# Where the stationary weights begin in memory, and in which order the k tiles come, in a two-layer hybrid block on one core

## The chip, the core and the metric

The kernel runs on one core of a Trainium2 chip. The metric is the time of one execution on the device in microseconds (us); the median of several runs counts.

## What is computed

The reference is a block of two layers on 16 meta tokens and 256 tokens of input, 272 together, with a model width of 1024. The zero tokens that pad the sequence to a multiple of 128 in front do not count. In short:

```
for li in range(2):
    hn = rms_norm(h)                       # 272 x 1024
    proj = hn @ w_in[li]                   # 1024 x 13312, split into 12 parts
    o = retention(..), hgrn2(..), diff_attention(..)      # three branches, each 272 x 1024
    y = sum(sigmoid(mg) * (branch @ w_branch[li]))        # three products 1024 x 1024
    h = h + y @ w_out[li]                                 # 1024 x 1024
    u = rms_norm(h) @ w_ffn_in[li]         # 1024 x 5632, then a convolution of width 3 in time
    h = h + (silu(gate) * val) @ w_ffn_out[li]            # 2816 x 1024
out = rms_norm(h)[the 256 input tokens]
```

All is float32. The weights of both layers are some 212 MB and are read once.

## The kernel before

**Products.** Nearly all of TensorE's time goes into the weight products. Features lie on the partitions and tokens in the free dimension, so a weight tile of 128 x 128 is the stationary operand, and the moving operand is a k tile of the activations: 128 features by 272 tokens in layer 0. In layer 1 the last tokens alone matter for the outputs, so most products there move 258 tokens, from token 14 on, which is 56 bytes further (`T0 = 14`). The names in `FULL` (`rk`, `rv`, `hf`, `hi`, `dk`, `dv`) move all 272 there too. To keep float32 accuracy, weights and activations are each cut into a high and a low part of type fp32r, and each weight tile takes three matmuls: `whi` by the high activations (L873), `whi` by the low ones (L874), `wlo` by the high ones (L875). I call these three a triple below.

**Order of tiles.** A product is named by its group and a pair number `j`: `("fi", 3)` makes the output tiles f=0 and f=1 of pair 3. `ORDER` writes out by hand which product follows which, with the background work between. `_turns` turns that into the list of weight tiles: for every k tile in rising order the two columns f=0 and f=1, so 16 triples for the eight k tiles of a product. `fo` has 22 k tiles; its pair 3 runs all k of column 0, then all k of column 1.

- Products of the input projection (`BASE`, 52 pairs a layer, 30 of them short in layer 1) and of the feed-forward input (`fi`, 22 pairs) move the tiles `xh` and `xl`. These are 320 words a k tile apart, so all k tiles begin at the same place modulo 256 bytes: 0, or 56 for the short ones.
- The branch products (`b0`, `b1`, `b2`, 4 pairs each), the output product (`wo`, 4 pairs) and the feed-forward output (`fo`, 4 pairs, layer 0) move tiles cut out of "slots" of four k tiles by 272 words. 272 words are 1088 bytes, so the start moves on by 64 bytes modulo 256 with every k.
- The feed-forward output of the last layer (`final`) is the other way around: 128 tokens of `ghi` and `glo` are stationary and 512 columns of the weights move (L1383 to L1385). There are 22 k tiles, two token tiles and two column halves, three matmuls each: 264 matmuls.

**Weights.** `_Weights.next` brings the weight tiles in chunks of eight, in the order of use: one DMA into `wraw` (3 buffers), one copy on ScalarE into `whi` (rounding to fp32r), one subtraction on VectorE into `wlo` (4 buffers each). `_places` says at which word of `whi` and `wlo` each tile begins. The tile pools put `whi` and `wlo` at 64 modulo 256 and the slots at 64 modulo 256. So a place of 0 means a weight that begins at 64 modulo 256.

**Places before.** Below, the *distance* is the start of the weight minus the start of the moving operand, modulo 256 bytes. In before it is 64 for all of `BASE` with 272 columns, 104 for `BASE` with 258 columns, and 64 (layer 0) or 104 (layer 1) for `b0`, `b1`, `b2`, `wo` and `fo` pairs 0 to 2. For `fi` it is spread by `SPREAD`: pair j has 64 + 16 j for j up to 15, and 72, 112, 152, 192, 232, 16 for the pairs 16 to 21, in both layers alike. In `fo` pair 3 and in `final` the tiles are packed without a wanted place, so the distance takes all of 0, 64, 128 and 192 in turn.

**Order of work.** `_Plan` simulates the engines with a cost for each instruction and writes out the order of all engines; products are its backbone, and the retention, hgrn2 and attention heads are spread behind them. In the feed-forward stage, `Norm.next` makes the normalised `xh` and `xl` anew after four pairs (`DEFER`), while the first pairs are scaled after the product.

Of the kernel before, what the change touches and what calls it, by code (L numbers as in the profile page):

```python
# [19 lines left out]
P = 128  # L20
DEPTH = 2
# [61 lines left out]
def _ktiles(name):  # L83
    return FK if name == "fo" else KD


def _turns(li):

    pairs = [x for x in ORDER if x[0][0] not in MARKS]
    if li == DEPTH - 1:
        pairs = [x for x in pairs if x[0] != "fo"]
    groups = [[x] for x in pairs]
    if li == 0:
        groups[:2] = [pairs[:2]]
    turned = [[x] for n in (BASE, ("fi",)) for x in [x for x in pairs if x[0] in n][DEFER - 1 : DEFER]]
    out = []
    for group in groups:  # L100
        if group == [("fo", 3)]:
            out.append([("fo", 3, k, f) for f in range(2) for k in range(FK)])
        else:
            nk = _ktiles(group[0][0])
            out.append([x + (k, f) for k in range(nk // 2) for x in group for f in range(2)])
            out[-1] += [x + (k, f) for x in group for k in range(nk // 2, nk) for f in range(2)]
            if group in turned:
                out[-1] = out[-1][nk:] + out[-1][:nk]
    if li == DEPTH - 1:
        out.append([("fo", j, k, f) for k in range(FK) for j in range(KD // 2) for f in range(2)])  # L110
    return out
# [12 lines left out]
WIDE = 320  # L124


def _places(depth=DEPTH):

    wants = []
    for li in range(depth):
        for name, j, k, _ in sum(_turns(li), []):
            if name == "fo" and (li == DEPTH - 1 or j == 3):
                wants.append(None)
                continue
            short = li == DEPTH - 1 and name not in FULL
            if name in BASE or name == "fi":
                wants.append((SPREAD[j] + 4 * T0 * short if name == "fi" else APART[short]) % LINE)
                continue  # L140
            wants.append(APART[short] + BLOCK * (name[0] == "b" or name in ("wo", "fo")) + 64 * (k % 4))
    out = []
    for c in range(0, len(wants), CHUNK_TILES):
        at, places = 0, []
        for want in wants[c : c + CHUNK_TILES]:
            if want is not None:
                at += (want // 4 - at) % (LINE // 4)
            places.append(at)
            at += P
        assert at <= ROOM  # L150
        out.append(places)
    return out


def _runs(places):


    runs = []
    for i, at in enumerate(places):
        if runs and at == runs[-1][1] + runs[-1][2] * P:  # L160
            runs[-1][2] += 1
        else:
            runs.append([i, at, 1])
    out = []
    for i, at, n in runs:
        if out and out[-1][4] == n and (out[-1][3] == 1 or at == out[-1][1] + out[-1][2] * out[-1][3]):
            if out[-1][3] == 1:
                out[-1][2] = at - out[-1][1]
            out[-1][3] += 1
        else:  # L170
            out.append([i, at, 0, 1, n])
    return out


# [20 lines left out]
def _stream(w_in, w_branch, w_out, w_ffn_in, w_ffn_out):  # L195

    out = np.empty((DEPTH, STREAM, P, P), np.float32)
    for li in range(DEPTH):
        tiles = sum(_turns(li), [])
        for i, (name, j, k, f) in enumerate(tiles):  # L200
            if name in BASE:
                w, cols = w_in[li], _columns(name, BASE[name] + 2 * j + f)
            elif name in ("b0", "b1", "b2"):
                w, cols = w_branch[li][int(name[1])], _columns(name, 2 * j + f)
            elif name == "wo":
                w, cols = w_out[li], _columns(name, 2 * j + f)
# [6 lines left out]
    out = out.reshape(n, CHUNK_TILES, P, P).transpose(0, 2, 1, 3)  # L213
    return np.ascontiguousarray(out).reshape(n, P, CHUNK_TILES * P)


# [346 lines left out]
class _Weights:  # L563
# [6 lines left out]
        self.used = 0  # L570
        self.places = _places()

    def part(self, t, at, step, runs, n):

        return bass.AP(t.tensor, t.offset + at, [list(t.ap[0]), [max(step, 1), runs], [1, n * P]])

    def next(self):
        c, i = divmod(self.used, CHUNK_TILES)
        self.used += 1
        if i == 0:  # L580
            due = self.plan.key
            room = [P, ROOM]
            raw = self.plan.tile(self.pool, [P, CHUNK_TILES * P], F32, "wraw", 3, f"wraw{c}")
            hi = self.plan.tile(self.pool, room, F32R, "whi", 4, f"whi{c}")
            lo = self.plan.tile(self.pool, room, F32R, "wlo", 4, f"wlo{c}")
            self.plan.key = due - LEAD
            pieces = 1 if c > 1 else 2
            for p in range(pieces):
                n = CHUNK_TILES // pieces
                cols = slice(p * n * P, (p + 1) * n * P)  # L590
                self.sp.dma_start(raw[:, cols], self.w[c][:, cols])
                for first, at, step, runs, each in _runs(self.places[c][p * n : (p + 1) * n]):
                    src = raw[:, (p * n + first) * P : (p * n + first + runs * each) * P].rearrange("p (r x) -> p r x", r=runs)
                    self.act.activation(self.part(hi, at, step, runs, each), src, AF.Copy)
                    self.dve.tensor_tensor(out=self.part(lo, at, step, runs, each), in0=src, in1=self.part(hi, at, step, runs, each).bitcast(F32), op=SUB)
            self.plan.key = due
            self.cut = hi, lo
        hi, lo = self.cut
        at = self.places[c][i]
        return hi[:, at : at + P], lo[:, at : at + P]  # L600

    def chunk(self):

# [13 lines left out]
def _trace(ctx, tc, plan, a, depth, probe):  # L617
# [114 lines left out]
    def x_tile(k, folded):  # L732
        return tuple(t[:, k % 4, :] for t in xs[1 if k >= 4 else 2 if folded else 0])
# [43 lines left out]
    class Norm:  # L777
# [42 lines left out]
        def next(self):  # L820

            self.pairs += 1
            if self.pairs != DEFER + 1:
                return
            self.folded = True
            ys = []
            for k in range(KD):
                plan.key = clock[0] - 12.0 + 0.3 * k
                if k % 4 == 0:
                    ys.append(slot4("y"))  # L830
                y = ys[-1][:, k % 4, :]
# [73 lines left out]
    def split(hi, lo, x):  # L905
        act.activation(hi, x, AF.Copy)
        tt(lo, x, hi.bitcast(F32), SUB)
# [40 lines left out]
    for li in range(depth):  # L948
# [402 lines left out]
        def final():  # L1351
# [21 lines left out]
            for k, t, c in order:  # L1373
# [33 lines left out]
        for name, j in ORDER:  # L1407
# [111 lines left out]
                    norm.finish()  # L1519
            elif name == "fi":  # L1520
                ps = products(lambda k: x_tile(k, norm.folded), name, j, t0)
                if j % 4 == 0:
# [6 lines left out]
                first = META if last else 0  # L1529
                c = temp2("two_b")  # L1530
                for f in range(2):
                    ft = j + f * FK
# [9 lines left out]
                split(st["ghi"][j // 4][:, j % 4, first:], st["glo"][j // 4][:, j % 4, first:], c[:, 0, :])  # L1542
            elif last:
                if j == 0:
                    final()
# [37 lines left out]
```

## Time and profile before

| | |
|---|---|
| median of 3 runs | 1326.98 us (1326.49 to 1327.44) |
| the profiled execution's own time | 1326.42 us |
| its span, first to last instruction | 1324.6 us |
| TensorE matmuls busy | 1314.0 us, 99% |
| VectorE busy | 962.4 us, 73% |
| ScalarE busy | 816.4 us, 62% |
| DMA | 48.0% of 16 engines on the weights' queue |

A matmul's recorded duration is longer than the time from its start to the next one's, since matmuls are pipelined. So the pace is read from starts: two rows of the timeline and the count of triples between them. A span divided by that count is given below as ns a triple.

### The profile page before, as it was taken

The page shows a single profiled execution, that of the slowest core. Times are in us where ns is not written, and L with a number is a line of the kernel's source. Part 1 is how long each engine was busy: PE and PEld are TensorE (multiplying, and loading weights), DVE is VectorE, ACT ScalarE, POOL GpSimd, SP SyncE. Part 2 cuts the span into 40 slices and gives each one's busy share as a digit, 9 for nine tenths or more (in the row PEclk, how much of TensorE's full clock was granted, in tenths as well). Part 3 has the DMA queues.
Part 4 walks back from the last instruction along what each step waited for, and adds up shares of the span by engine and source line. Part 5 has one row for each costly group of instructions (what it writes and reads, how often), then busy time and mean ns, then how long its engine had stood idle before and what let it go on. Part 6 is the DMA issues. An engine that isn't in the chain of part 4 may idle for free.

```text
span 1324.6 us, 28929 instructions
## 1 busy us (share of the span) xinstructions
PE 1314.0 (99%) x11862; PEld 1285.7 (97%) x11862; DVE 962.4 (73%) x1630; ACT 816.4 (62%) x1374; POOL 83.2 (6%) x161
## 2 busy tenths in 40 slices
PE   9999999999999999999999999999999999999998
PEld 8999999999999999999999999999999999999986
DVE  7675777697585789886574757776985867898753
ACT  6847454756576566666456475547565865766643
POOL 5000000001010020000030000000011100200000
PEclk9999999999999999999999999999999999999999
DMA  7544543444544545555555445444445345365653
GB/s 272 194 150 153 172 148 132 140 144 139 181 143 152 183 144 183 183 170 181 175 176 187 149 159 173 148 144 144 148 140 183 136 165 201 131 211 185 204 182 107
DMA packets 60755, 219.07 MB, mean 165 GB/s; under 512 B 6864, under 2 KB 6992, under 8 KB 60624
## 3 DMA queue, kind: packets, MB, share of 16 engines
q1 hardware_dynamic: 60336, 216.71, 48.0%
q8 instruction: 93, 1.52, 0.5%
q10 hardware_dynamic: 288, 0.52, 0.1%
q14 instruction: 38, 0.31, 0.1%
HBM read 216.16 MB, written 1.05 MB: 164 GB/s over the span
## 4 chain that ended last, share of the span: by engine, by line
PE 95%; DVE 3%; ACT 1%; issue 0%; DMA 0%; SPq 0%; DVEq 0%
PE main L873 28%; PE main L875 27%; PE main L874 27%; PE fo L1383 2%; PE fo L1385 2%; PE fo L1384 2%; PE lev L1064 1%; DVE two_b L558 1%; PE ds L1248 1%; PE ms L558 1%; PE do L558 1%; PE ro L558 1%; PE ho L558 1%; PE vt L558 1%; DVE wlo L558 1%; PE s L558 0%
## 5 line engine op out<-in xcount | busy, mean ns | idle before, releaser
L873 PE MATMUL main<-xh,whi 128*128 128x272 f32 (+1 forms) x2368 | 691.8, 292 | 0.7 <-ACT whi L558 0.7
L875 PE MATMUL main<-xh,wlo 128*128 128x272 f32 (+1 forms) x2368 | 676.1, 286 | 1.0 <-DVE wlo L558 0.9
L874 PE MATMUL main<-xl,whi 128*128 128x272 f32 (+1 forms) x2368 | 675.7, 285 | 1.3 <-DVE xl L558 1.3
L558 DVE TENSOR_TENSOR wlo<-wraw,whi 128x1024 fp32r<-128x1024 f32 (+1 forms) x408 | 497.2, 1223 | 197.9 <-ACT whi L558 195.2
L558 ACT ACTIVATE whi<-wraw 128x1024 fp32r<-128x1024 f32 (+1 forms) x408 | 426.4, 1048 | 228.1 <-PE main L874 160.1
L873 PEld LDWEIGHTS main<-xh,whi 128*128 128x128 f32 x2368 | 446.1, 188 | 2.6 <-ACT whi L558 1.1
L874 PEld LDWEIGHTS main<-xl,whi 128*128 128x128 f32 x2368 | 446.1, 188 | 2.3 <-DVE xl L558 1.7
L875 PEld LDWEIGHTS main<-xh,wlo 128*128 128x128 f32 x2368 | 445.7, 188 | 2.4 <-DVE wlo L558 2.3
L558 DVE SCALAR_TENSOR_TENSOR two_b<-main,small,two_b 128x256 f32<-128x256 f32 (+2 forms) x144 | 65.4, 489 | 30.7 <-ACT two_b L558 29.0
L558 ACT ACTIVATE two_b<-main,small 128x272 f32<-128x272 f32 (+1 forms) x72 | 37.2, 566 | 29.6 <-PE main L875 29.6
L558 POOL TENSOR_TENSOR y<-h,rstd 128x272 f32<-128x272 f32 x32 | 34.5, 1113 | 317.7 <-ACT rstd L558 317.7
L875 PE MATMUL main<-ghi,wlo 128*128 128x272 f32 x176 | 51.0, 290 | 0.0
L873 PE MATMUL main<-ghi,whi 128*128 128x272 f32 x176 | 50.9, 289 | 0.0
L874 PE MATMUL main<-glo,whi 128*128 128x272 f32 x176 | 50.2, 285 | 0.0
L558 ACT ACTIVATE vsrc<-main 128x544 f32<-128x544 f32 x24 | 15.0, 625 | 38.5 <-PE main L875 38.4
L873 PE MATMUL main<-b0hi,whi 128*128 128x272 f32 (+1 forms) x128 | 38.2, 298 | 0.0
L873 PE MATMUL main<-b1hi,whi 128*128 128x272 f32 (+1 forms) x128 | 38.1, 298 | 0.0
L875 PE MATMUL main<-b2hi,wlo 128*128 128x272 f32 (+1 forms) x128 | 36.7, 286 | 0.0
L875 PE MATMUL main<-yhi,wlo 128*128 128x272 f32 (+1 forms) x128 | 36.7, 286 | 0.0
L875 PE MATMUL main<-b1hi,wlo 128*128 128x272 f32 (+1 forms) x128 | 36.6, 286 | 0.0
L875 PE MATMUL main<-b0hi,wlo 128*128 128x272 f32 (+1 forms) x128 | 36.6, 286 | 0.0
L873 PE MATMUL main<-b2hi,whi 128*128 128x272 f32 (+1 forms) x128 | 36.5, 285 | 0.0
(244 smaller groups left out, 1934.4 us busy)
## 6 DMA issues: line engine op xcount, KB each, us to landing
wraw<-in_w SPq DMA_DIRECT2D x402, 512.0 KB, 3.3
h<-in_h SPq DMA_DIRECT2D x4, 272.0 KB, 5.7
dec<-in_dec SPq DMA_DIRECT2D x2, 544.0 KB, 5.5
wraw<-in_w SPq DMA_DIRECT2D x4, 256.0 KB, 5.4
const<-in_const SPq DMA_DIRECT2D x1, 937.0 KB, 6.4
gain<-in_gl SPq DMA_DIRECT2D x1, 512.0 KB, 5.2
out<-y ACTq DMA_DIRECT2D x2, 256.0 KB, 2.8
out<-y SPq DMA_DIRECT2D x2, 256.0 KB, 2.7
```

What stands on the lines that cost most here:

```text
L558: self.plan.add(self.name, lambda: f(*args, **kw), cost, outs, ins, args[2] if method == "activation" else None)
L873: nc.tensor.matmul(o, wh, hi, start=first, stop=False)
L874: nc.tensor.matmul(o, wh, lo, start=False, stop=False)
L875: nc.tensor.matmul(o, wl, hi, start=False, stop=last)
L1064: nc.tensor.matmul(o, keys, x, start=True, stop=True)
L1248: nc.tensor.matmul(ss[m][:, at : at + nk], q[half, hd, q0 : q0 + P], k[half, hd, :nk], start=True, stop=True)
L1383: nc.tensor.matmul(o, gh, wh, start=False, stop=False)
L1384: nc.tensor.matmul(o, gl, wh, start=False, stop=False)
L1385: nc.tensor.matmul(o, gh, wl, start=False, stop=end)
```

## The change

1. All `fi` products get the distance that `BASE` has: 64 with 272 columns. `SPREAD` goes.
2. All short products of layer 1 (258 columns) get the distance 160: `BASE`, `fi`, `b0`, `b1`, `b2` and `wo`.
3. `b0`, `b1`, `b2`, `wo` and `fo` take their k tiles downward in blocks of four (3, 2, 1, 0, 7, 6, 5, 4, ...); `wo` ends with 5, 4, 7, 6. Going from one k to the next, the start of weight and moving operand goes back by 64 bytes instead of on by 64. `fo` pair 3 gets the distance 64 too.
4. In the last layer `ghi` and `glo` hold 256 tokens a k tile instead of 272, so that every stationary tile of `final` begins at 64 modulo 256 and the distance is 0 throughout.
5. The buffers of `whi` and `wlo` shrink from 4608 to 4352 bytes (both multiples of 256), and within a chunk the tiles are stored sorted by place, so that ScalarE and VectorE still write most chunks by one instruction.

```diff
+def _ks(name):
+    ks = list(range(_ktiles(name)))
+    if name in BASE or name == "fi":
+        return ks
+    blocks = [ks[i : i + 4][::-1] for i in range(0, len(ks), 4)]
+    if name == "wo":
+        blocks[-1] = [5, 4, 7, 6]
+    return sum(blocks, [])
...
-            out.append([("fo", 3, k, f) for f in range(2) for k in range(FK)])
+            out.append([("fo", 3, k, f) for f in range(2) for k in _ks("fo")])
...
-            out.append([x + (k, f) for k in range(nk // 2) for x in group for f in range(2)])
-            out[-1] += [x + (k, f) for x in group for k in range(nk // 2, nk) for f in range(2)]
+            ks = _ks(group[0][0])
+            out.append([x + (k, f) for k in ks[: nk // 2] for x in group for f in range(2)])
+            out[-1] += [x + (k, f) for x in group for k in ks[nk // 2 :] for f in range(2)]
...
-APART = (0, 96)
+BEGIN = 64
 BLOCK = 64
-ROOM = CHUNK_TILES * P + 2 * LINE // 4
+ROOM = CHUNK_TILES * P + LINE // 4
...
-SPREAD = [16 * i for i in range(16)] + [8 + 40 * i for i in range(6)]
+APART = (64, 160)
...
             if name in BASE or name == "fi":
-                wants.append((SPREAD[j] + 4 * T0 * short if name == "fi" else APART[short]) % LINE)
-                continue
-            wants.append(APART[short] + BLOCK * (name[0] == "b" or name in ("wo", "fo")) + 64 * (k % 4))
+                moving = [0, 0]
+            else:
+                moving = [BLOCK + 4 * T * (k % 4)] * 2
+            wants.append([APART[short] + 4 * T0 * short - BEGIN + x for x in moving])
...
+        if c // CHUNK_TILES > 1 and None not in mine:
+            order.sort(key=lambda i: mine[i][0] % LINE)
...
-                gh, gl = (x[k // 4][:, k % 4, tokens(t)] for x in (hi, lo))
+                gh, gl = (x[k // 4][:, k % 4, t * P : (t + 1) * P] for x in (hi, lo))
...
-                    st.setdefault("ghi", []).append(slot4("ghi", F32R))
-                    st.setdefault("glo", []).append(slot4("glo", F32R))
+                    for n in ("ghi", "glo"):
+                        g = slot(n, F32R)[:, : 4 * (T - first)]
+                        st.setdefault(n, []).append(g.rearrange("p (a t) -> p a t", a=4))
```

On TensorE, POOL and SP the order of instructions is row for row what it was (names and shapes; start addresses and the number of a k tile do not show there). On ScalarE and VectorE it is the same but for four chunks, all of them in layer 0's feed-forward output. On ScalarE, before, the chunks at the end of `fo` pair 2 and the beginning of pair 3 (`whi` is the rounded copy of a chunk's raw weights):

```order
L558 ACTIVATE whi_1213<-wraw_1212 128x4x256
L558 ACTIVATE whi_1216<-wraw_1215 128x256
L558 ACTIVATE whi_1216<-wraw_1215 128x768
L558 ACTIVATE whi_1222<-wraw_1221 128x1024
L558 ACTIVATE whi_1225<-wraw_1224 128x1024
```

And the same place after:

```order
L589 ACTIVATE whi_1213<-wraw_1212 128x4x256
L589 ACTIVATE whi_1216<-wraw_1215 128x2x128
L589 ACTIVATE whi_1216<-wraw_1215 128x2x256
L589 ACTIVATE whi_1216<-wraw_1215 128x2x128
L589 ACTIVATE whi_1222<-wraw_1221 128x4x256
L589 ACTIVATE whi_1225<-wraw_1224 128x4x256
```

The chunk 1216 is written in three pieces instead of two, and the chunks of pair 3 behind it in four blocks with gaps of 64 bytes by one instruction; their neighbours stay. On VectorE the same chunks, before (`wlo` is the subtraction):

```order
L558 TENSOR_TENSOR wlo_1214<-wraw_1212,whi_1213 128x4x256
L558 TENSOR_TENSOR wlo_1217<-wraw_1215,whi_1216 128x256
L558 TENSOR_TENSOR wlo_1217<-wraw_1215,whi_1216 128x768
L558 TENSOR_TENSOR wlo_1223<-wraw_1221,whi_1222 128x1024
L558 TENSOR_TENSOR wlo_1226<-wraw_1224,whi_1225 128x1024
L558 TENSOR_TENSOR h_78<-h_78,main_1199 128x544
```

And after:

```order
L589 TENSOR_TENSOR wlo_1214<-wraw_1212,whi_1213 128x4x256
L589 TENSOR_TENSOR wlo_1217<-wraw_1215,whi_1216 128x2x128
L589 TENSOR_TENSOR wlo_1217<-wraw_1215,whi_1216 128x2x256
L589 TENSOR_TENSOR wlo_1217<-wraw_1215,whi_1216 128x2x128
L589 TENSOR_TENSOR wlo_1223<-wraw_1221,whi_1222 128x4x256
L589 TENSOR_TENSOR wlo_1226<-wraw_1224,whi_1225 128x4x256
L589 TENSOR_TENSOR h_78<-h_78,main_1199 128x544
```

The pieces are the same as on ScalarE. In all, each of the two engines has three instructions more; the same bytes are written.

More of the change, by code (lines that the diff above doesn't have):

```diff
@@ L117 @@
 LINE = 256
[L118 removed]
+BEGIN = 64
 BLOCK = 64
[L120 removed]
+WIDE = 320
+ROOM = CHUNK_TILES * P + LINE // 4
 T0 = META - 2
 FULL = ("rk", "rv", "hf", "hi", "dk", "dv")
[L123 to L124 removed]
+APART = (64, 160)
 def _places(depth=DEPTH):
@@ L133, in _places @@
         for name, j, k, _ in sum(_turns(li), []):
-            if name == "fo" and (li == DEPTH - 1 or j == 3):
+            if name == "fo" and li == DEPTH - 1:
                 wants.append(None)
@@ L145, in _places @@
[L145 to L151, printed above, removed]
-    return out
[L155 to L171, printed above, removed]
+        mine = wants[c : c + CHUNK_TILES]
@@ new lines, in _places @@
+        order, places = list(range(CHUNK_TILES)), [[0] * CHUNK_TILES for _ in range(2)]
+        if c // CHUNK_TILES > 1 and None not in mine:
+            order.sort(key=lambda i: mine[i][0] % LINE)
+        for part in range(2):
+            at = 0
+            for i in order:
+                if mine[i] is not None:
+                    at += (mine[i][part] // 4 - at) % (LINE // 4)
+                places[part][i] = at
+                at += P
+            assert at <= ROOM, at
+        out.append((order, places))
@@ new lines, in _places, with _boxes, box @@
+    return out
+def _boxes(*places):
+    def box(first, n):
+        for inner in (n, 2, 1):
+            if n % inner:
+                continue
+            dims = []
+            for at in places:
+                at = at[first : first + n]
+                one = at[1] - at[0] if inner > 1 else P
+                two = at[inner] - at[0] if inner < n else 0
+                if one < 1 or two < 0 or any(at[i] != at[0] + i // inner * two + i % inner * one for i in range(n)):
+                    break
+                dims.append((at[0], two, one))
+            if len(dims) == len(places):
+                return first, n // inner, inner, dims
+        return None
+    out, first, end = [], 0, len(places[0])
+    while first < end:
+        found = next(x for n in range(end - first, 0, -1) if (x := box(first, n)))
+        out.append(found)
+        first += found[1] * found[2]
@@ L212, in _stream @@
     n = DEPTH * STREAM // CHUNK_TILES
-    out = out.reshape(n, CHUNK_TILES, P, P).transpose(0, 2, 1, 3)
+    out = out.reshape(n, CHUNK_TILES, P, P)
+    out = np.stack([out[c, order] for c, (order, _) in enumerate(_places())])
+    out = out.transpose(0, 2, 1, 3)
     return np.ascontiguousarray(out).reshape(n, P, CHUNK_TILES * P)
@@ L571, in __init__, with part @@
         self.places = _places()
-    def part(self, t, at, step, runs, n):
-        return bass.AP(t.tensor, t.offset + at, [list(t.ap[0]), [max(step, 1), runs], [1, n * P]])
+    def part(self, t, at, two, one, outer, inner):
+        return bass.AP(t.tensor, t.offset + at, [list(t.ap[0]), [max(two, 1), outer], [one, inner], [1, P]])
     def next(self):
@@ L591, in next @@
                 self.sp.dma_start(raw[:, cols], self.w[c][:, cols])
[L592 to L595, printed above, removed]
+                order, places = self.places[c]
+                mine = [[x[i] for i in order[p * n : (p + 1) * n]] for x in places]
+                for first, outer, inner, dims in _boxes(*mine):
+                    src = self.part(raw, (p * n + first) * P, inner * P, P, outer, inner)
+                    to_hi, to_lo = (self.part(t, *x, outer, inner) for t, x in zip((hi, lo), dims))
+                    self.act.activation(to_hi, src, AF.Copy)
+                    self.dve.tensor_tensor(out=to_lo, in0=src, in1=to_hi.bitcast(F32), op=SUB)
             self.plan.key = due
             self.cut = hi, lo
-        hi, lo = self.cut
-        at = self.places[c][i]
-        return hi[:, at : at + P], lo[:, at : at + P]
+        return tuple(t[:, at[i] : at[i] + P] for t, at in zip(self.cut, self.places[c][1]))
     def chunk(self):
@@ L1521, in _trace @@
                 ps = products(lambda k: x_tile(k, norm.folded), name, j, t0)
+                first = META if last else 0
                 if j % 4 == 0:
-                    st.setdefault("ghi", []).append(slot4("ghi", F32R))
-                    st.setdefault("glo", []).append(slot4("glo", F32R))
+                    for n in ("ghi", "glo"):
+                        g = slot(n, F32R)[:, : 4 * (T - first)]
+                        st.setdefault(n, []).append(g.rearrange("p (a t) -> p a t", a=4))
                 u = ps
@@ L1528, in _trace @@
                     evacuate(u, ps)
-                first = META if last else 0
                 c = temp2("two_b")
@@ L1541, in _trace @@
                 tt(c[:, 0, :], c[:, 0, :], c[:, 1, :], MUL)
-                split(st["ghi"][j // 4][:, j % 4, first:], st["glo"][j // 4][:, j % 4, first:], c[:, 0, :])
+                split(st["ghi"][j // 4][:, j % 4, :], st["glo"][j // 4][:, j % 4, :], c[:, 0, :])
             elif last:
```

1 line of the change is left out of this document (removed).

## The prediction

> **What bounds the kernel now.** I read the page first, then the chain of waits, then the starts of matmuls in the timeline.
>
> ```profile
> span 1324.6 us, 28929 instructions
> PE 1314.0 (99%) x11862; PEld 1285.7 (97%) x11862; DVE 962.4 (73%) x1630; ACT 816.4 (62%) x1374; POOL 83.2 (6%) x161
> PEclk9999999999999999999999999999999999999999
> PE 95%; DVE 3%; ACT 1%; issue 0%; DMA 0%; SPq 0%; DVEq 0%
> PE main L873 28%; PE main L875 27%; PE main L874 27%; PE fo L1383 2%; PE fo L1385 2%; PE fo L1384 2%; PE lev L1064 1%; DVE two_b L558 1%; PE ds L1248 1%; PE ms L558 1%; PE do L558 1%; PE ro L558 1%; PE ho L558 1%; PE vt L558 1%; DVE wlo L558 1%; PE s L558 0%
> ```
>
> TensorE's own work is 95% of the chain that sets the end, at full clock, and the three matmuls of a triple are 82% of it. So a nanosecond taken from every triple counts in full, except where another engine holds the chain. The number of matmuls and columns does not change here; what can change is the pace. The next rows are starts of TensorE's matmuls; between two of them lies a known number of triples.
>
> ```profile
> 685.92 0.28 PE L873 MATMUL main<-xh,whi 128*128 128x272 f32 x1
> 709.61 0.29 PE L873 MATMUL main<-xh,whi 128*128 128x258 f32 x1
> 732.24 0.28 PE L873 MATMUL main<-xh,whi 128*128 128x272 f32 x1
> ```
>
> These are `hf` (272 columns, distance 64) and then `hg` (258 columns, distance 104) in layer 1, four pairs or 64 triples each, with nothing between: 23.69 / 64 = 370.2 ns and 22.63 / 64 = 353.6 ns a triple. The `fi` products have the same shapes and other distances:
>
> ```profile
> 517.08 0.28 PE L873 MATMUL main<-xh,whi 128*128 128x272 f32 x1
> 547.25 0.29 PE L873 MATMUL main<-xh,whi 128*128 128x272 f32 x1
> 553.27 0.29 PE L873 MATMUL main<-xh,whi 128*128 128x272 f32 x1
> 607.62 0.29 PE L873 MATMUL main<-ghi,whi 128*128 128x272 f32 x1
> 1138.46 0.28 PE L873 MATMUL main<-xh,whi 128*128 128x258 f32 x1
> 1144.22 0.28 PE L873 MATMUL main<-xh,whi 128*128 128x258 f32 x1
> 1157.67 0.28 PE L873 MATMUL main<-xh,whi 128*128 128x258 f32 x1
> 1163.47 0.28 PE L873 MATMUL main<-xh,whi 128*128 128x258 f32 x1
> 1169.07 0.29 PE L873 MATMUL main<-xh,whi 128*128 128x258 f32 x1
> 1238.17 0.28 PE L873 MATMUL main<-xh,whi 128*128 128x258 f32 x1
> ```
>
> In layer 0, pairs 7 to 21 (240 triples) run from 517.08 to 607.62: 377.3 ns a triple, 7.1 more than at distance 64. Pair 12 alone (547.25 to 553.27, distance 0) takes 376.3. In layer 1, pairs 5 to 18 (224 triples, 1157.67 to 1238.17) take 359.4; pair 5 (distance 144) takes 362.5, pair 6 (1163.47 to 1169.07, distance 160) takes 350.0, pair 2 (1138.46 to 1144.22, distance 96) takes 360.0. The work around these pairs on the other engines is the same, and the distance alone differs. So the distance sets the pace, by up to 12 ns a triple, and the two distances that the change gives (64 with 272 columns, 160 with 258) are the fast ones seen.
>
> The Trainium skill's page "TensorE: Matmul & The Clock Gate" (section "Step-by-step: what each phase is for") says that TensorE has two independent read ports into its memory, one for the moving operand and one for weights, and that loading the next weights takes no bandwidth from the running matmul. By it no start address would matter and the sum below would be 0. The rows 350.0 and 362.5 for equal shapes speak against it; it stands below as a rival.
>
> **The change part by part.** The sum is made against the profiled execution's 1326.42 us, of which 1324.6 is span; it lies 0.56 below the median of 1326.98.
>
> *`fi`, layer 0.* Here other engines hold the chain for a while:
>
> ```profile
> 482.84 0.15 PE main L874
> 483.01 1.07 ACT whi L558
> 503.77 1.15 DVE wlo L558
> 504.96 0.39 PE main L875
> 1135.56 0.13 PE main L874
> 1135.71 1.07 ACT whi L558
> 1153.96 0.42 DVE xl L558
> 1154.43 0.39 PE main L874
> ```
>
> and in the list of waits:
>
> ```profile
> PE main L874 <- DVE xl L558: 1.3, 1, 1.3
> ```
>
> The chain of waits goes through ScalarE and VectorE from 483.0 to 505.0, where VectorE makes `wlo`, the convolutions and the new `xl` one behind the other. A faster TensorE only waits longer there, so what is gained between is lost. Pairs 6 to 21 come behind it: 256 triples x 7.1 = 1.8 us. Before 483.0 lie pair 0, which has distance 64 already, and some 9 triples of pair 1: at up to 10 ns 0.1. Together 1.9.
>
> *`fi`, layer 1.* The chain is off TensorE from 1135.7 to 1154.4, with an open wait of 1.3 us for `xl`. Before that lie pair 0 (distance 64) and half of pair 1; I take the 10 ns of pair 2 for pair 0: 0.2 us. Behind it come pairs 5 to 21, 272 triples, from 359.4 to 350.0: 2.6 us. Just after the wait there is something else:
>
> ```profile
> 1155.14 0.31 PE L873 MATMUL main<-xh,whi 128*128 128x258 f32 x1
> 1157.53 0.30 PE L875 MATMUL main<-xh,wlo 128*128 128x258 f32 x1
> ```
>
> 18 matmuls of pair 4 (distance 128), the first and last of which are shown, start 2.39 / 17 = 141 ns apart, against 117 at distance 160. The clock is full there; this distance has a second, slower pace into which the long wait has thrown it. Without it, 18 x 24 = 0.4 us. Together 3.2 us; I keep 3.1, since the last pairs have some other work between.
>
> *`BASE` with 258 columns.* 30 pairs x 16 = 480 triples, from 353.6 to the 350.0 of pair 6 of `fi`, whose residues are exactly theirs after: 1.7 us. Some of these triples have background matmuls between (`lev`, `ds`, `ro` and others in the chain's lines), where the pace starts anew; I take 1.5. The single pair of 16 triples is all that bears this price, so its ends are 0 and 1.9.
>
> *`b0` to `b2`, `wo` and `fo`, steady part and steps.* Here each k has two triples (f=0, f=1), then comes a step to the next k.
>
> ```profile
> 425.61 0.29 PE L873 MATMUL main<-b2hi,whi 128*128 128x272 f32 x1
> 473.50 0.28 PE L873 MATMUL main<-xh,whi 128*128 128x272 f32 x1
> 1080.62 0.29 PE L873 MATMUL main<-b2hi,whi 128*128 128x258 f32 x1
> 1126.59 0.28 PE L873 MATMUL main<-xh,whi 128*128 128x258 f32 x1
> ```
>
> `b2` and `wo` (128 triples in each layer) take 47.89 / 128 = 374.1 ns in layer 0 and 45.97 / 128 = 359.1 in layer 1. Against the steady 370.2 and 353.6 at the same distances, a step costs twice the difference: 7.8 and 11.0 ns. In a step upward the next weight, which is loaded while the last matmul of the old k runs, lies 128 (layer 0) or 168 (layer 1) from that matmul's moving operand; downward it lies at 0 or 96. No row of before shows a downward step. Its lower price is that one matmul at the pace of these distances: (376.3 - 370.2) / 3 = 2.0 and (360.0 - 350.0) / 3 = 3.3 ns; as the upper one I set twice today's, 16 and 22. I take the middle of the lower price and today's, 5 and 7, since the distance in the step is a better one but the step stays a break. Layer 0 has 16 pairs x 8 + 3 pairs x 22 = 194 steps: 194 x 2.8 = 0.5 us (ends 1.1 and -1.6). Layer 1 has 256 triples and 128 steps: from 359.1 to 350.0 + 3.5 = 353.5, so 256 x 5.6 = 1.4 us (ends 1.9 and -0.5). In `fo` pair 3 the spread distances go and every triple has a step: I set 0.1.
>
> The new order makes nothing late: the halves of `y` and the blocks of four are finished together, and `wo` still reaches k 6 and 7 as its last four triples. The weights come in the same chunks at the same times, so SP's queue is not touched.
>
> *`final`.* Its 22 k tiles have 12 matmuls each; the distance goes 64, 128, 192, 0 and again.
>
> ```profile
> 1257.12 0.39 PE L1383 MATMUL fo<-whi,ghi 128*128 128x512 f32 x1
> 1265.46 0.39 PE L1383 MATMUL fo<-whi,ghi 128*128 128x512 f32 x1
> 1268.19 0.40 PE L1383 MATMUL fo<-whi,ghi 128*128 128x512 f32 x1
> 1301.41 0.40 PE L1383 MATMUL fo<-whi,ghi 128*128 128x512 f32 x1
> ```
>
> k 0 to 15 (192 matmuls) take 44.29 / 192 = 230.7 ns each; k 3, at distance 0, takes 2.73 / 12 = 227.5. At distance 0 throughout: 264 x 3.2 = 0.8 us (ends 0.5 and 0.9).
>
> *Writing the weights.* Three more instructions on each of ScalarE and VectorE, all in `fo` of layer 0, where the page has these two busy to 73% and 62% and TensorE waits for neither: nothing. If that cover were gone, each would cost no more than the fixed part of such an instruction, some tenths of a microsecond. The pools keep their residues, since the buffers shrink by 256 bytes.
>
> The sum: 1.9 + 3.1 + 1.5 + 0.5 + 1.4 + 0.1 + 0.8 = 9.3 us, so 1317.1 for a profiled execution and **1317.7 us** for the median.
>
> **The rivals.**
>
> (a) *The 160 does not carry over.* The good pace of one pair of `fi` is its own, and `BASE`, the branch products and `wo` in layer 1 keep what they have. For it: distance 104 gives 353.6 in `hg` but 359.1 where k steps. Against it: within `fi` the paces of 64 and of 160 hold over all 16 triples, and `BASE` gets the same bytes of both operands. Loss 1.5 + 1.4: 1320.6 us. Chance 0.15.
>
> (b) *The feed-forward stages turn VectorE-bound.* TensorE asks for weights 2 to 3% sooner, and the waits of 483 to 505 and 1136 to 1154 come again. Against it: behind 505 and 1154.4 the chain is TensorE's. If all of `fi`'s 5.0 us went back: 1322.7 us. Chance 0.07.
>
> (c) *Slower: downward steps lock the slow pace.* The 141 ns above show that a distance can hold a run at 24 ns a matmul more once it is thrown in. If each downward step did that for the two triples of its k, 6 x 24 = 144 ns would come on each of 322 steps, 46 us: with 11 us of gains in the other parts some 1362 us. The point from which it decides: the other parts bring 1.9 + 3.1 + 1.5 + 0.8 = 7.3, and free steps would bring 2.9 more and the steady part of layer 1 0.9; steps of more than some 35 ns eat all of it. Against it: no clean run of products shows more than 11 ns a step. Chance 0.03.
>
> (d) *Addresses do not matter*, and something else set those paces: 1327.0 us, no change. Against it are the rows; for it nothing here. Chance 0.02. This is what the Trainium skill's page named above would give.
>
> **How the numbers follow.** The forecast has 0.73. The range takes in (a), the ends of the steps, and half of (b) below: gains of 4.5 to 12 us, 1315.0 to 1322.5. What a measurement of this kernel can tell from no change is some 0.2%, 2.7 us: faster than that in the forecast, (a), (b) and most of what lies between, 0.93; within it 0.04 ((d) and a costly step); slower 0.03 (c).
>
> **What would show it.** In the profile after, `fi` of layer 0 should run at 370 ns a triple, `fi` and `BASE` of layer 1 at 350, `b2` and `wo` at 372 to 373 and near 353.5, `final` at 227.5 a matmul; the wait for `xl` in layer 1 should grow from 1.3 to some 1.7 us (10 ns on some 40 triples of pairs 1 to 4 before it), and the run at 141 ns should be gone. I am wrong if `b2` and `wo` stand above 374 and 359, or if `BASE` with 258 columns stays at 353.6.

## The result, and the profile after

| | before | after |
|---|---|---|
| median | 1326.57 us (1326.30 to 1327.44, 6 runs) | 1318.11 us (1317.66 to 1318.42, 6 runs) |
| ratio, 95% interval | | 0.9937 [0.9927, 0.9947] |
| the profiled execution's own time | 1326.42 us | 1318.42 us |
| its span | 1324.6 us | 1316.6 us |

The changed kernel is faster by 8.5 us; the prediction for its median was 1317.7. From the page after, the span, the engines, the granted clock and the chain by engine:

```profile
span 1316.6 us, 28935 instructions
PE 1305.5 (99%) x11862; PEld 1278.1 (97%) x11862; DVE 962.9 (73%) x1633; ACT 816.9 (62%) x1377; POOL 83.5 (6%) x161
PEclk9999999999999999999999999999999999999999
PE 96%; DVE 2%; ACT 1%; DMA 0%; issue 0%; SPq 0%; DVEq 0%
```

The same 11862 matmuls at the same full clock take 8.5 us less of TensorE's time; VectorE and ScalarE have three instructions more each and are otherwise where they were. The next rows are starts of TensorE's matmuls in the changed kernel, at the places that the prediction showed of before, with the first column the start in us.

```profile
425.15 0.28 PE L905 MATMUL main<-b2hi,whi 128*128 128x272 f32 x1
472.86 0.29 PE L905 MATMUL main<-xh,whi 128*128 128x272 f32 x1
516.34 0.29 PE L905 MATMUL main<-xh,whi 128*128 128x272 f32 x1
605.14 0.29 PE L905 MATMUL main<-ghi,whi 128*128 128x272 f32 x1
682.98 0.29 PE L905 MATMUL main<-xh,whi 128*128 128x272 f32 x1
706.67 0.28 PE L905 MATMUL main<-xh,whi 128*128 128x258 f32 x1
729.07 0.29 PE L905 MATMUL main<-xh,whi 128*128 128x272 f32 x1
1076.04 0.28 PE L905 MATMUL main<-b2hi,whi 128*128 128x258 f32 x1
1098.60 0.28 PE L905 MATMUL main<-yhi,whi 128*128 128x258 f32 x1
1121.35 0.28 PE L905 MATMUL main<-xh,whi 128*128 128x258 f32 x1
1157.87 0.28 PE L905 MATMUL main<-xh,whi 128*128 128x258 f32 x1
1158.13 0.39 PE L907 MATMUL main<-xh,wlo 128*128 128x258 f32 x1
1163.65 0.28 PE L905 MATMUL main<-xh,whi 128*128 128x258 f32 x1
1250.20 0.40 PE L1415 MATMUL fo<-whi,ghi 128*128 128x512 f32 x1
1293.73 0.39 PE L1415 MATMUL fo<-whi,ghi 128*128 128x512 f32 x1
```

Paces first. `fi` of layer 0, pairs 7 to 21: 88.80 us for 240 triples, 370.0 ns (377.3 before). `hf`, whose distance was not changed: 23.69 / 64 = 370.2, as before. `hg`: 22.40 / 64 = 350.0 (353.6). `b2` and `wo` of layer 0 together: 47.71 / 128 = 372.7 (374.1). In layer 1 `b2` has 22.56 / 64 = 352.5 and `wo` 22.75 / 64 = 355.5 (both together 359.1). `final`, k 0 to 15: 43.53 / 192 = 226.7 a matmul (230.7).

Then the stretches between these rows, against the same ones of before. The eight microseconds of the span lie in them as follows:

| stretch | before | after | gain | predicted |
|---|---|---|---|---|
| start to `fi` of layer 0 | 473.50 | 472.86 | 0.64 | some 0.3 (steps) |
| `fi` of layer 0 | 134.12 | 132.28 | 1.84 | 1.9 |
| `fo` of layer 0, start of layer 1 | 78.30 | 77.84 | 0.46 | some 0.3 (steps, pair 3) |
| `hf` to the last product before `b2`, layer 1 | 394.70 | 393.06 | 1.64 | 1.5 + 0.7 |
| `b2`, `wo`, layer 1 | 45.97 | 45.31 | 0.66 | 0.7 |
| `fi` of layer 1 | 130.53 | 128.85 | 1.68 | 3.1 |
| `final` to the end of the span | 67.48 | 66.40 | 1.08 | 0.8 |
| sum | 1324.6 | 1316.6 | 8.0 | 9.3 |

The predicted column divides the 1.4 of layer 1's `b0` to `b2` and `wo` by halves, and the 0.5 + 0.1 of layer 0 likewise. The gain of the first row is not the change's; the same start of `BASE` products in both profiles, before and after:

```profile
35.30 0.29 PE L873 MATMUL main<-xh,whi 128*128 128x272 f32 x1
```

```profile
34.67 0.28 PE L905 MATMUL main<-xh,whi 128*128 128x272 f32 x1
```

Up to here no distance has changed, and after is already 0.63 us ahead: scatter of the start. Some 0.2 of it is lost again among products of layer 0 that the change does not touch, so that 0.4 is left at the start of `b1`; `b2` and `wo` brought 47.89 - 47.71 = 0.18 by themselves. So of the 8.0 some 7.6 is the change's.

The waits of TensorE in the changed kernel (in us: total, times, longest):

```profile
PE main L906 <- DVE xl L589: 2.0, 2, 1.6
PE main L907 <- DVE wlo L589: 0.8, 3, 0.3
```

In before the wait for `xl` was 1.3 in one piece. The run at 141 ns behind it is gone, and another thing stands there: from 1157.87 to 1163.65 the sixteen triples of pair 6 take 361 ns each, with a late matmul at 1158.13, and the pairs after it do not come back to 350 in this execution: they run at 353.

### The profile page after: what moved, and what is told of

Same layout as the page of the kernel before. It is cut to its first block, busy times and chain, and to the rows that moved or that the text cites. A ratio compares the mean times of both kernels' runs of the same rounds, so it can differ in the third digit from the quotient of the medians.

```text
span 1316.6 us, 28935 instructions
## 1 busy us (share of the span) xinstructions
PE 1305.5 (99%) x11862; PEld 1278.1 (97%) x11862; DVE 962.9 (73%) x1633; ACT 816.9 (62%) x1377; POOL 83.5 (6%) x161
## 4 chain that ended last, share of the span: by engine, by line
PE 96%; DVE 2%; ACT 1%; DMA 0%; issue 0%; SPq 0%; DVEq 0%
PE main L905 28%; PE main L907 27%; PE main L906 27%; PE fo L1417 2%; PE fo L1416 2%; PE fo L1415 2%; PE lev L1096 1%; PE ds L1280 1%; PE ms L589 1%; PE do L589 1%; PE ro L589 1%; PE ho L589 1%; PE vt L589 1%; DVE two_b L589 1%; DVE wlo L589 1%; PE s L589 0%
## 5 line engine op out<-in xcount | busy, mean ns | idle before, releaser
L905 PE MATMUL main<-yhi,whi 128*128 128x272 f32 (+1 forms) x128 | 36.4, 284 | 0.0
L906 PE MATMUL main<-b0lo,whi 128*128 128x272 f32 (+1 forms) x128 | 36.4, 284 | 0.0
L906 PE MATMUL main<-b1lo,whi 128*128 128x272 f32 (+1 forms) x128 | 36.4, 284 | 0.0
```

The source lines that it names most:

```text
L905: nc.tensor.matmul(o, wh, hi, start=first, stop=False)
L906: nc.tensor.matmul(o, wh, lo, start=False, stop=False)
```

## The experiments

**Steps upward again** (e1_up): the k tiles of the branch products, `wo` and `fo` rise as in before; all distances stay.

```diff
-    blocks = [ks[i : i + 4][::-1] for i in range(0, len(ks), 4)]
-    if name == "wo":
-        blocks[-1] = [5, 4, 7, 6]
-    return sum(blocks, [])
+    return ks
```

> The changed kernel with all k tiles in rising order again; distances stay 64 and 160. Theory (what the next weight's distance is in a step sets the step's cost): b2 and wo in layer 0 go back from 372.5 and 372.9 to about 374.1 ns a triple; in layer 1 the next weight lies 224 from the moving operand in a step instead of 96, and the one upward step that wo has now shows triples of 365 beside 353, so b2 and wo come to 356 to 358. Together 1.2 to 1.8 us slower than the changed kernel's 1318.1: 1319.3 to 1319.9. Rival (the direction is nothing, all the gain there came from the steady distance): b2 stays at 372.5 and 352.5, 1318.1.

Measured 1319.81 us (1318.73 to 1320.56), ratio 0.9949 [0.9934, 0.9963]: 1.7 us behind the change. The starts of `b2`, of the `fi` behind `wo` (layer 0), then of `b2`, `wo` and `fi` (layer 1):

```profile
424.69 0.29 PE L902 MATMUL main<-b2hi,whi 128*128 128x272 f32 x1
472.57 0.28 PE L902 MATMUL main<-xh,whi 128*128 128x272 f32 x1
1076.69 0.28 PE L902 MATMUL main<-b2hi,whi 128*128 128x258 f32 x1
1099.57 0.28 PE L902 MATMUL main<-yhi,whi 128*128 128x258 f32 x1
1122.55 0.28 PE L902 MATMUL main<-xh,whi 128*128 128x258 f32 x1
```

Layer 0 has 47.88 / 128 = 374.1 ns again, exactly before's. In layer 1 `b2` has 357.5: of the 6.6 ns that the change brings there (359.1 to 352.5), the distance gives 1.6 and the direction 5.0. The intervals of the two kernels overlap, so it is these rows that carry the reading. Over all products whose order changed (`b0` to `b2`, `wo`, `fo`), the times from one product's first start to the next one's add up to some 1.7 us more in this profile than in the change's.

**The activations of `BASE` and `fi` 32 bytes further** (e2_x32): the distance becomes 32 with 272 columns and 128 with 258; the branch products keep theirs.

```diff
-    ... F32R)[:, :, :T] for n in "hl"] for i in range(3)]
+    ... F32R)[:, :, 8 : 8 + T] for n in "hl"] for i in range(3)]
```

> The changed kernel with the tiles xh and xl moved on by 32 bytes, all weights where they are: distance 32 for 272 columns and 128 for 258 columns in BASE and fi, nothing else changed. Theory (the distance sets the pace): 1536 triples go from 370 to 380 ns (15 us more), and the 832 short ones from 350 to 357 at least (6 us), or to 3 x 141 = 422 where the slow pace of distance 128 is locked (up to 60 us). So 1339 us at least and up to 1393. Rival (the weight's own start modulo 256, or nothing about addresses, counts): 1318.

Measured 1362.52 us (1362.15 to 1362.90), 44 us above the change. `hf`, `hg` and what follows, then the first pair of `fi` in layer 1, two matmuls of the norm behind it, and what comes then up to `final`:

```profile
690.43 0.28 PE L905 MATMUL main<-xh,whi 128*128 128x272 f32 x1
714.74 0.28 PE L905 MATMUL main<-xh,whi 128*128 128x258 f32 x1
737.46 0.28 PE L905 MATMUL main<-xh,whi 128*128 128x272 f32 x1
...
1145.13 0.28 PE L905 MATMUL main<-xh,whi 128*128 128x258 f32 x1
...
1150.82 0.62 PE L589 MATMUL ms<-sum,ones_d 128*128 128x272 f32 x2
1151.07 0.48 PE L905 MATMUL main<-xh,whi 128*128 128x258 f32 x1
...
1293.96 0.41 PE L1415 MATMUL fo<-whi,ghi 128*128 128x512 f32 x1
```

`hf` runs at 379.8 ns (370.2 in the change), `hg` at 355.0 (350.0). Pair 0 of `fi` has 355 to 356 too (1145.13 to 1150.82). Behind the two `ms` matmuls the same distance runs at 420 ns, 140 a matmul, from 1151 to the end: 336 triples in 142.89 us, 425 with what lies between them. `fi` of layer 1 takes 148.8 us, 20.0 more than in the change. So 32 bytes cost 44 us at full clock, and a distance alone does not name a pace: 128 has one of 355 and one of 420. The same holds with 272 columns: at distance 32, where `hf` has 379.8, pairs 7 to 21 of `fi` in layer 0 run at 376.0 (521.82 to 612.06, 240 triples).

**Activations and weights both 32 bytes further** (e3_both32): as e2, and the wanted starts of these weights too (`moving = [32, 32]`).

> The changed kernel with xh and xl and the weights of BASE and fi all moved on by 32 bytes: distances 64 and 160 as in the changed kernel, other residues. Theory (only the distance counts): 370 and 350 ns a triple as before, 1318.1 +- 0.6 us. Rival (the residues themselves count, 0 and 64): the pace leaves 370 and 350; by the spread seen in fi up to 12 ns a triple on 2368 triples, up to 28 us more.

Measured 1318.29 us (1318.19 to 1318.85), ratio 0.9939 [0.9924, 0.9953], and the paces are back:

```profile
682.85 0.29 PE L905 MATMUL main<-xh,whi 128*128 128x272 f32 x1
706.53 0.28 PE L905 MATMUL main<-xh,whi 128*128 128x258 f32 x1
728.93 0.29 PE L905 MATMUL main<-xh,whi 128*128 128x272 f32 x1
```

370.0 and 350.0. At this one shift of both, neither operand's own start matters; the difference does.

**Distance 104 for all short products** (e8_104): `APART = (64, 104)`, the distance of before, with the new order of k and the rest of the change. This is rival (a) put to the test, and the price of 160 over 104.

> The changed kernel with distance 104 instead of 160 for all short products of layer 1, k tiles still downward. Theory: hg at 353.6 and fi at 353.5 again (480 and 352 triples x 3.5 ns: 1.5 + 0.9 us, less where fi was at 353.6 in the changed kernel anyway); b2 and wo with steps to 40: 355 to 360, 0.6 to 1.9 us. Together 2 to 4 us slower than the changed kernel: 1320 to 1322. Rival a of the prediction (160 does not carry over): no change, 1318.1.

Measured 1323.11 us (1320.68 to 1324.12, 7 runs), ratio 0.9972 [0.9961, 0.9982], 4.7 us above the changed kernel beside it on the same chip. `fi` of layer 1 from pair 6 on, up to the matmuls that stand between its last triples, 253 triples:

```profile
1161.05 0.28 PE L905 MATMUL main<-xh,whi 128*128 128x258 f32 x1
...
1253.06 0.27 PE L589 MATMUL fo<-const,h 128*128 128x128 f32 x1
```

92.01 / 253 = 363.7 ns, where the same distance gives 353.6 in `hg`. Here again one distance has two paces. The expectation had 353.5 for `fi`, and the time came out above its 1320 to 1322: so the 4.7 us hold the distance and a slower draw of it together. The single times spread by 3.4 us, more than any other kernel's; that the slower pace is drawn in some executions only would explain most of it (256 triples by 10 ns are 2.6 us), but only the slowest of them was profiled.

**One pair of `fi` in layer 1 at distance 144** (e4_pair8) was to break the pace that the first profile after shows from 1157.87 on.

```diff
+            if (li, name, j) == (DEPTH - 1, "fi", 8):
+                moving = [-16, -16]
```

> The changed kernel with pair 8 of fi in layer 1 alone at distance 144 instead of 160. In the changed kernel fi of layer 1 ran at 350 ns a triple until a wait of 0.1 us for wlo at 1158 us, and at 353.6 from there on to the end of fi. Theory (the wait threw the run into a second pace of the same distance, which holds until something breaks it): pairs 6 and 7 at 353.6, pair 8 at some 362, pairs 9 to 21 at 350: 208 x 3.5 - 16 x 9 = 0.6 us faster than the changed kernel, 1317.5. Rival (VectorE and ScalarE, at 80 to 90% there, slow TensorE's reads): pairs 9 to 21 stay at 353.6, 0.15 us slower, 1318.3.

Measured 1318.26 us (1317.68 to 1319.01), but pair 7, and pair 6 behind its late matmul, already ran at 350 here, so there was nothing to break: inconclusive on that. It shows that pair 8 pays for its distance (5.70 us, 356 ns a triple) and that the pairs behind it do not (352 for the next one, then 350).

**The changed kernel once more** (e9_again), no edit, profiled anew.

> The changed kernel itself once more. Theory (the 353.6 of fi in layer 1 was a chance of that execution, set off by a wait of 0.1 us): another profile shows fi of layer 1 at 350 for part or all of its pairs, and single times spread by up to 0.9 us between executions, 1317.5 to 1318.5. Rival (the fi stage runs at 353.6 whenever its VectorE is that busy): 353.6 again behind 1158 us, and single times agree within 0.3 us.

Measured 1318.40 us (1317.85 to 1318.98, 5 runs). Pair 7 of `fi` in layer 1 and the start of `final`:

```profile
1164.96 0.28 PE L905 MATMUL main<-xh,whi 128*128 128x258 f32 x1
1250.73 0.40 PE L1415 MATMUL fo<-whi,ghi 128*128 128x512 f32 x1
```

85.77 us, where the first profile after has 86.55. The 353 of the first profile was that execution's draw: e1, e3, e4 and e11, whose `fi` has the same distances (but for pair 8 in e4), ran these pairs at 350 as well. This execution is not shorter for it (span 1317.1): its first products began 0.5 us later, and in layer 1 TensorE stood still once before a level of `hgrn2`, as the list of waits says:

```profile
PE lev L1096 <- issue: 0.6, 1, 0.6
```

That wait, of 0.6 to 1.2 us, stands in most of the experiments' profiles and in neither of the first two. What ends it does not show.

**One pair at distance 160 amid the 420** (e7_break): as e2, and pair 8 and one tile of pair 14 of `fi` in layer 1 brought to 160.

```diff
+            if (li, name) == (DEPTH - 1, "fi") and (j == 8 or (j, k, f) == (14, 7, 1)):
+                moving = [32, 32]
```

> The kernel with x moved by 32 bytes (distance 128 for short products, where fi of layer 1 fell into 420 ns a triple after its first interruption and stayed there for 330 triples, while hg at the same distance ran at 355), and in fi of layer 1 pair 8 whole and one single tile of pair 14 (k 7, f 1) back at distance 160. Theory (a pace is held until a different distance breaks it, and what comes after is a new draw): pair 8 at some 350, and the pairs behind it at 355 with some chance, at 420 else; the same behind the tile of pair 14. If both breaks lead to 355: 13 pairs x 16 x 65 ns = 13 us less than the 1362.5 us. Rival (the engines beside it or the fi stage itself make 420): everything but pair 8 stays at 420, 1361.4 us.

Measured 1362.51 us (1362.13 to 1362.88). Pair 8:

```profile
1198.93 0.31 PE L907 MATMUL main<-xh,whi 128*128 128x258 f32 x1
1205.65 0.31 PE L907 MATMUL main<-xh,whi 128*128 128x258 f32 x1
```

6.72 / 16 = 420 ns at distance 160, which ran at 350 or 353 in the profiles without the shift. Here a better distance did not end the held pace, and the pairs behind the single tile of pair 14 stay at 420 as well: my theory was wrong.

**Other matmuls amid the 420** (e10_matmul): as e2, and behind pairs 6, 10, 14 and 18 of that `fi` an extra float32 matmul of 128, 64, 32 and 96 columns into a bank that nothing reads. In TensorE's order the first of them comes earlier than in the program: 80 triples of `fi` stand before it, so it lies behind pair 4.

```diff
+BREAKS = {6: 128, 10: 64, 14: 32, 18: 96}
+                if last and j in BREAKS:
+                    ...
+                    pe.matmul(bank("break")[:, : BREAKS[j]], ones_d, ones_d[:, : BREAKS[j]], start=True, stop=True)
```

> The kernel with x moved by 32 bytes again (distance 128, fi of layer 1 held at 420 ns a triple from its pair 1 on, neither a pair nor a tile at distance 160 let it go), with one extra float32 matmul that nobody reads behind pairs 6, 10, 14 and 18 of fi in layer 1, of 128, 64, 32 and 96 columns. Theory (420 is a phase between weight load and stream that holds until the stream is interrupted; each interruption is a new draw): at least one of the four changes the pace, to 355 or back; each stretch at 355 saves 64 x 65 ns = 4.2 us, so the time lies between 1362.5 and 1346. Rival (the fi stage of layer 1 makes 420, whatever runs between): 420 throughout, 1363 us.

One time, 1357.02 us, 5.5 below e2. Each extra matmul (its record, or one of its two, shown) and the first `fi` matmul behind it:

```profile
1179.27 0.27 PE L590 MATMUL break<-ones_d 128*128 128x128 f32 x1
1179.41 0.37 PE L906 MATMUL main<-xh,whi 128*128 128x258 f32 x1
...
1219.72 0.22 PE L590 MATMUL break<-ones_d 128*128 128x64 f32 x1
1219.86 0.37 PE L906 MATMUL main<-xh,whi 128*128 128x258 f32 x1
...
1246.78 0.30 PE L590 MATMUL break<-ones_d 128*128 128x32 f32 x2
1246.92 0.37 PE L906 MATMUL main<-xh,whi 128*128 128x258 f32 x1
...
1269.72 0.24 PE L590 MATMUL break<-ones_d 128*128 128x96 f32 x1
```

From 1219.86 to 1246.78, 64 triples: 420.6 ns. From 1246.92 to 1269.72, 64 triples: 356.3. The break of 128 columns and that of 64 left 420 as it was, that of 32 ended it, and the one of 96 did not bring it back. So in this one execution a foreign matmul ended the held pace and two others did not, and the stage of `fi` does not force 420 by itself. Why the third one ended it is open.

**More distances** (e6_map): each pair of `fi` gets another one, in steps down to 4 bytes.

```diff
+DISTANCE = [8, 24, 40, 56, 88, 104, 120, 136, 148, 156, 164, 168, 172, 184, 200, 216, 248, 68, 60, 76, 92, 84]
+            if name == "fi":
+                wants.append([4 * T0 * short + DISTANCE[j] - BEGIN] * 2)
+                continue
```

> The changed kernel with fi spread over distances that no run has shown (steps of 8 and some of 4 bytes; 8, 24, 40, 56, 88, 104, 120, 136, 148, 156, 164, 168, 172, 184, 200, 216, 248, 68, 60, 76, 92, 84 for pairs 0 to 21, both layers). Theory: each pair has a pace of its own by its distance, 370 to 383 ns in layer 0 and 350 to 363 in layer 1; on average 376 and 358, so some 1.8 + 2.4 = 4 us over the changed kernel, 1322. If some distance gives less than 370 or 350, it is a better one. Rival (the paces of distances 64 and 160 are the best by chance of the run): no order, the same distance classes vary as much as the others.

One time, 1322.57 us. None beats the two distances of the change: the lowest are 370.1 (distance 92, 272 columns) and 350.9 (172, 258 columns). Pair 17 (distance 68) of layer 0 and its end:

```profile
576.67 0.29 PE L909 MATMUL main<-xh,whi 128*128 128x272 f32 x1
582.76 0.29 PE L909 MATMUL main<-xh,whi 128*128 128x272 f32 x1
```

6.09 / 16 = 380.6 ns: four bytes off the 64 of the change cost 10 ns. This is one pair in one execution, and a held pace is not ruled out for it; before's pair 16, at distance 72, has 370.8.

**`wo` in plain fours** (e11_wo): the line that ends `wo` with 5, 4, 7, 6 goes, so that every step inside a four is downward.

> The changed kernel with wo in plain fours downward (3, 2, 1, 0, 7, 6, 5, 4) instead of ending with 5, 4, 7, 6. Theory (an upward step costs more): wo in layer 1 goes from 355.4 to 352.5 ns a triple (0.2 us) and loses its triples of 365. But k 7 and 6 then come four triples sooner, at some 452.0 us in layer 0, while the low part of y for them was finished at 453.0 before: a new wait of some 1 us on TensorE at wo in each layer. Net 1 to 1.8 us slower. Rival (the order at the end of wo is free): no wait, 0.2 us faster.

One time, 1319.0 us (with 1.2 us of the wait at `lev`). `wo` of layer 1 runs from 1100.14 to 1122.78:

```profile
1100.14 0.28 PE L903 MATMUL main<-yhi,whi 128*128 128x258 f32 x1
1104.84 0.28 PE L904 MATMUL main<-ylo,whi 128*128 128x258 f32 x1
1122.78 0.28 PE L903 MATMUL main<-xh,whi 128*128 128x258 f32 x1
```

22.64 / 64 = 353.8 ns against 355.5, worth 0.1 us, too little to be told in a time. I had expected TensorE to wait for the last `ylo`, and it did not. In the order of the instructions, the planner puts five triples of `wo`'s second pair between the two halves of the first, so that the half with k 4 to 7 begins 13 triples in, at 1104.72. VectorE's last `ylo` (the low part of `y`) is done by then:

```profile
1102.82 0.69 DVE L587 TENSOR_TENSOR ylo<-y,yhi 128x516 fp32r<-128x516 f32 x1
```

No experiment gave a version whose time can be told from the changed kernel's for the better.

## Why the prediction held, step by step

*The time came closer than the sum.* The forecast missed the median by 0.4 us, and that is partly luck: it counted 9.3 us down from before's 1326.98, while the six runs of before have 1326.57 and the gain is 8.5. In the two profiles the gain is 8.0, of which 7.6 is the change's.

*The distance sets the pace.* Shown from both sides: e3 moves both operands and nothing changes, e2 moves one, `hf` goes from 370.0 to 379.8 and `hg` from 350.0 to 355.0, and the kernel is slower by 44 us. Rival (d) is out. The held pace comes on top of it, and the prediction had it only as a loss at distance 128 and in rival (c). The Trainium skill's page "TensorE: Matmul & The Clock Gate" (section "Step-by-step: what each phase is for") says that loading the next weights takes no bandwidth from the running matmul. To read from it that start addresses are free is wrong in this case: 350.0 and 355.0 ns in `hg` for equal shapes and counts speak against that. Whether it is bandwidth that they cost, no run here shows.

*The 160 carries over.* `hg`, the one clean stretch of short `BASE` products, has 350.0, as predicted from a single pair of `fi`; e8 prices 160 over 104 at 4.7 us in all, a slower draw of 104 in `fi` included. Rival (a) is out. The term was still too large: 1.64 us came in the stretch for which I had 1.5 + 0.7. Of these, `b0` and `b1` gave 0.42 instead of 0.7, and the short `BASE` products 1.2; with 0.14 of the first `hq` behind `fo`, `BASE` has some 1.4 of 1.5. Of the products with background matmuls between their triples, `m0` gained nothing (30.41 us before, 30.42 after), while `m1` gained 0.22, as much as the clean run of `hg` with as many triples (0.23). Why some gain and others do not is not shown.

*The steps.* The price was taken between a floor and today's. Layer 0: 2 x (372.7 - 370.2) = 5.0 ns a step, where I had set 5. Layer 1, `b2`: 2 x (352.5 - 350.0) = 5.0, where I had set 7. `wo` alone stands higher, at 355.5, and its ending has a step upward; without that ending (e11) it has 353.8, so this explains some of it. The rest is open, since e11 has five triples of the second pair between the halves of the first. e1 shows that it is the direction. Rival (c) did not come about: no step locked anything. But its mechanism, a held pace of 140 ns, is real, and cost e2 its 44 us in good part.

*`final`.* Every matmul has 226.7 ns, a little below the one k on which the estimate rested (227.5): 1.08 us with the end, predicted 0.8.

*`fi` of layer 1 is the term that was mis-sized*: 3.1 predicted, 1.68 measured. These 1.4 us are most of the gap between the predicted 9.3 and the 7.6 that the change brought. It failed in two places. First, I took the chain to be TensorE's from pair 5 on. Pairs 0 to 6 took 42.30 us after 42.48: 0.18 gained where my terms held 0.8 to 0.9. TensorE came earlier, waited longer for `xl` (2.0 in all, where I had set some 1.7), and what the 141-ns run had cost was then paid as waits for VectorE's `xl` and `wlo` and as the uneven paces around them: rival (b), in small and in this place only. Second, pairs 7 to 21 gained 88.05 - 86.55 = 1.50 us in this execution, and 88.05 - 85.77 = 2.28 in e9, where I had 2.3. That part of the estimate was right for e9 and for the others that ran at 350 (e1, e3, e11); the first profiled execution had drawn a slower pace, pairs 7 to 21 at some 353 instead of 350. The median does not show this draw by itself, since the start and the wait at `lev` scatter by as much.

*Writing the weights* cost nothing that shows: VectorE's and ScalarE's busy time went up by 0.5 us each, and the stretch with layer 0's `fo` became shorter by 0.46.

## What to carry to other kernels

Where one stream of short matmuls with a new weight each bounds the kernel, compare the pace of equal shapes over the whole trace by starts and counts; if it differs, print where both operands begin modulo 256 and look at the difference. Choose that difference by measured runs that are long and follow an interruption, since a distance that is good in one clean stretch (104: 353.6, 128: 355) can be held at 364 or 420 elsewhere. A nanosecond won just ahead of another engine's wait is not won, so count such triples only from where the chain has come back.

## What the runs showed that I had not expected

- A stream of weight load and matmul keeps a pace: with 258 columns 350 or 353 ns a triple at distance 160, 353.6 or 364 at 104, 355 or 420 at 128, in each case held over 64 triples or more (the slower of the two over more than 200), at full granted clock.
- The held pace can be stronger than the distance. At 160, which ran at 350 elsewhere, a pair amid a run of 420 had 420 (e7). Waits and foreign matmuls are where it changes (behind the `ms` matmuls in e2, behind the one of 32 columns in e10, at a late `wlo` in the first profile after); not all of them change it. A step to another distance can change it too (before's pairs 5 and 6 of `fi` in layer 1: 362.5, then 350.0) and need not (e7). What in the hardware holds it, no run here shows.
- Four bytes of distance went with 10 ns a triple in the one pair that had them (64: 370, 68: 381).
